# A hybrid two-layer block: split weights of the mixer and the recurrent stage kept in DRAM between the halves of the tokens

## Chip, cores and metric

The kernel runs on one core of a Trainium2 chip. The metric is the device time of one execution in microseconds (us). Engines are named PE (TensorE, with PEld for its weight loads), DVE (VectorE), ACT (ScalarE), POOL (GpSimd) and SP (SyncE, which here issues all DMAs).

## What is computed

Two layers on x of 1024 tokens by 1024 features, all in float32. Layer 0 has a mixer with two groups of heads (a gated delta rule and RWKV-7), layer 1 a gated linear recurrence; each is followed by a gated feed-forward network. Each sublayer has its norm and its AdaLN shift, scale and gate.

```python
def reference(x, c, ...):
    for layer in range(DEPTH):
        shift, scale, gate = adaln_params(c, ada_w[layer, 0], ada_b[layer, 0])
        h = rms_norm(x, norm_pre[layer, 0]) * (1.0 + scale) + shift
        if layer % 2 == 0:
            y = delta_rwkv_mixer(h, mix_w_in[j], mix_w_out[j], ...)
        else:
            y = rglru_mixer(h, lru_w_in[j], ..., lru_wa[j], ..., lru_wx[j], ..., lru_w_out[j])
        x = x + gate * rms_norm(y, norm_post[layer, 0])
        shift, scale, gate = adaln_params(c, ada_w[layer, 1], ada_b[layer, 1])
        h = rms_norm(x, norm_pre[layer, 1]) * (1.0 + scale) + shift
        y = swiglu_ffn(h, ffn_w_gate[layer], ffn_w_up[layer], ffn_w_down[layer])
        x = x + gate * rms_norm(y, norm_post[layer, 1])
    return x

def rglru_mixer(h, w_in, conv_w, conv_b, wa, ba, wx, bx, lam, w_out):
    gate_branch, xb = jnp.split(h @ w_in, 2, axis=-1)
    xb = causal_depthwise_conv(xb, conv_w) + conv_b
    r = sigmoid(einsum('btnd,nde->btne', xb, wa) + ba)
    i = sigmoid(einsum('btnd,nde->btne', xb, wx) + bx)
    ...
    return (hs * gelu(gate_branch)) @ w_out
```

## The kernel before

Every large product is done in three passes with operands split in two: a matrix w is taken as wh, its cast to the type float32r, and wl = w - wh, and the product is wh·xh + wh·xl + wl·xh, three matmuls of 128x128 by 512 columns (`gemm_steps`, or `prod` in `down`).

The weights are split in `load_w`. For each tile of 128 x 512 numbers (256 KB: four blocks of 128x128 side by side, two of 128x256, or one of 128x512) it lets SP load the raw tile into a buffer wf or wd (L135), lets ACT cast it to wh (L138), and POOL or DVE subtract to wl (L139). In the mixer POOL subtracts; in the recurrent stage DVE does it for the first tile of a product and POOL for the second; in the output products DVE does. wh and wl have three buffers each in the whole program. The raw tiles have two buffers wf in the mixer, and after `deepen` eight (two wf, six wd). A tile's buffers come free when PE has done its 12 matmuls.

The tokens go in two halves of 512, h = 0 and h = 1; each half loads and splits every weight again. The stages, in the order of time: `start` (AdaLN of the first norm), `mixer` (16 groups, a half and a head group each, of which three are at work at a time: the input products `proj` of one group, the chunk algebra of the one before, the serial chain of the one before that), the output product `mix_out` of h = 0 in the middle of the second half's groups and that of h = 1 at the end; the feed-forward stage of layer 0, both halves at once, and its product `down`; the recurrent stage `lru` with h = 0, its output through `down`, then h = 1 and its output; the feed-forward stage of layer 1. In `lru` four blocks follow one another: two input products (bank "mm"), a convolution, the two gate products with wa and wx, two products of the gate branch (bank "sb"), and the recurrence, most of it on DVE.

`proj` takes two tiles (24 matmuls), a gate product one; `down` takes one tile for each of 128 rows of the weight and each half of the columns, and `mix_out` and `lru` both use it. So the mixer has 60 input tiles and 16 output tiles in each half, and the recurrent stage 32 + 8 and 16.

Who runs what in which order on an engine is set by a scheduler that orders the recorded instructions by a model of their times; the order in the program is its starting point. Each engine, SP too, then works through its list in order: an instruction that waits holds up all behind it on that engine. Beside the weights, SP's list has loads of activations (L527), stores of results (L605), rows of AdaLN weights for the next stages (L500), and intermediate values of the feed-forward stages.

The store that the change copies exists already: the feed-forward stage puts its split product in DRAM through `gpart` (L769, L770) and loads it back with `load_g` (L804).

```python
wf = self.t(next(self.wtags), [128, step, n])[:, :m]
nc.sync.dma_start(wf, w[k0 * 128:(k0 + m) * 128, c0:c0 + n].rearrange("(k p) c -> p k c", p=128))
wh = self.t(tag or "wh", [128, step, n], F32R)[:, :m]
wl = self.t(tag or "wl", [128, step, n], F32R)[:, :m]
nc.scalar.copy(wh, wf)
(nc.gpsimd if self.pool_lo and (self.pool_lo > 1 or k0) else nc.vector).tensor_tensor(wl, wf, wh, ALU.subtract)
```

Of the kernel before, what the change touches and what calls it, by code (L numbers as in the profile page):

```python
# [10 lines left out]
F32 = mybir.dt.float32  # L11
# [4 lines left out]
ALU = mybir.AluOpType  # L16
# [4 lines left out]
KD = D // 128  # L21
# [51 lines left out]
class Block:  # L73
# [53 lines left out]
    def load_w(self, w, c0, nk=KD, n=128, tag=None):  # L127

        nc = self.nc
        step = 512 // n  # L130
        out = []
        for k0 in range(0, nk, step):
            m = min(step, nk - k0)
            wf = self.t(next(self.wtags), [128, step, n])[:, :m]
            nc.sync.dma_start(wf, w[k0 * 128:(k0 + m) * 128, c0:c0 + n].rearrange("(k p) c -> p k c", p=128))  # L135
            wh = self.t(tag or "wh", [128, step, n], F32R)[:, :m]
            wl = self.t(tag or "wl", [128, step, n], F32R)[:, :m]
            nc.scalar.copy(wh, wf)  # L138
            (nc.gpsimd if self.pool_lo and (self.pool_lo > 1 or k0) else nc.vector).tensor_tensor(wl, wf, wh, ALU.subtract)  # L139
# [40 lines left out]
    def run(self):  # L180
        nc, a = self.nc, self.a
# [12 lines left out]
        self.gd = self.dram("gd", 2 * NF * 2 * 128, 512)  # L194
        self.cd = self.dram("cd", 2 * (PRE + MID) * 128, 512)
# [380 lines left out]
    def down(self, lhs, w, h, x_in, x_out, Gb, banks, xtag="yx", tail=(None, 0), keep=False, aside=None):  # L576
# [37 lines left out]
        for half in range(2):  # L614
            ps = [self.t(banks[4 * half + t], [128, 512]) for t in range(4)]
            held = []
            for k in range(nk):
# [5 lines left out]
                wp, = self.load_w(w[k * 128:(k + 1) * 128], half * 512, 1, 512, ttag if late else None)  # L623
# [184 lines left out]
    def lru(self, h, hs):  # L808
# [16 lines left out]
        def branch(b):  # L825
            out = []
            for m in (2 * b, 2 * b + 1):
                ps = self.now(self.proj(w, 1024 + 128 * m, hs))
# [7 lines left out]
        for b in range(4):  # L836
# [5 lines left out]
            wb = [self.load_w(a[wn][0, b], 0, 2, 256) for wn in ("lru_wa", "lru_wx")]  # L842
# [8 lines left out]
            for i, m in enumerate(ms):  # L851
                z = self.t("cy", [128, 512])
                ps = self.now(self.proj(w, 128 * m, hs, "sb"))
# [24 lines left out]
    def layers(self, hs, AB, x1, x2, x3, late):  # L878
# [4 lines left out]
        for n, (l, x_in, x_out) in enumerate(subs):  # L883
# [20 lines left out]
            for h in range(2):  # L904
# [24 lines left out]
                def aside():  # L929
# [3 lines left out]
                    elif n + 1 < len(subs):  # L933
# [6 lines left out]
                               "s2" if keep else "yx", ("cy", 6) if keep else ("ht", 7) if last else (None, 0), keep, aside)  # L940
# [74 lines left out]
    def mix_out(self, h, x, x_out, mT, Gb, banks):  # L1015
# [12 lines left out]
        if h == 0:  # L1028
            self.down(lhs, self.a["mix_w_out"][0], h, x, x_out, Gb, banks)
        else:  # L1030
            return self.down(lhs, self.a["mix_w_out"][0], h, x, x_out, Gb, banks, "s2", ("cy", 6), True)
# [103 lines left out]
    def gdn_inputs(self, w, hs, i, h):  # L1135
        nc = self.nc
        out = []
        for n in range(3):
            ps = (yield from self.proj(w, 512 * n + 128 * i, hs))
# [14 lines left out]
        ps = (yield from self.proj(w, 1536 + 128 * i, hs))  # L1154
# [179 lines left out]
    def rwkv_lora(self, w, hs, h):  # L1334
        nc = self.nc
        wdad = self.shifted((yield from self.proj(w, 2056 + 1536, hs)), 24, 12, h, "st")
# [215 lines left out]
```

## Time and profile before

| | us |
|---|---|
| median of 3 runs | 2824.09 |
| lowest and highest | 2818.7, 2838.25 |
| the profiled execution | 2831.3 |
| its span in the trace | 2829.2 |

The execution's own time is 2.1 us longer than the span, which runs from the first to the last recorded instruction. All times of rows are us from the start of the span. In the profile all matmuls have line L98 or, for transposes, L101, since helpers record them; they are told apart by their tiles. A wait is named by the instruction that ended it. PEclk is the granted share of TensorE's full clock.

### The profile page before, as it was taken

Reading aid. Unit: us, or ns where it says so; the run is one execution under the profiler, and the core shown is the slowest. Engines: PE = TensorE matmul, PEld = TensorE weight load, DVE = VectorE, ACT = ScalarE, POOL = GpSimd, SP = SyncE. Lnnn points to the kernel's source line nnn. Section 1 sums busy time; section 2 is a strip of 40 time slices with the busy share of each in tenths; the row PEclk is TensorE's granted clock in tenths of the full one; section 3 lists DMA queues with packets and bytes.
Section 4 is the critical chain, followed back from the end, with each engine's and each line's share of the span. In section 5 each row is a group of like instructions: output and inputs, shape, how many; then the busy total and the mean of one; then the engine's idle time right before and its main releaser. Section 6 shows DMA issues by size and latency. Waiting matters only on the chain. (4 is left out here: it accounts for less than half of the span.)

```text
span 2829.2 us, 43760 instructions
## 1 busy us (share of the span) xinstructions
PE 2655.3 (94%) x16104; PEld 2050.8 (72%) x16104; DVE 1854.8 (66%) x3280; ACT 1258.1 (44%) x2302; POOL 662.9 (23%) x516
## 2 busy tenths in 40 slices
PE   6899999998999998899999999999998899999998
PEld 3666666666766766677888878777776688888887
DVE  5867778677677655998454463997974885544233
ACT  4555565554555535333332232664755333333222
POOL 2322221232322105232330000211215333331000
PEclk9999999999999999899999999999999999999999
DMA  7412222224511154766447874635334454448753
GB/s 236 120 44 54 61 79 61 68 56 138 159 53 53 58 186 149 223 215 209 139 145 282 291 253 126 189 116 160 112 110 150 149 195 149 142 134 287 232 187 108
DMA packets 402653, 415.75 MB, mean 147 GB/s; under 512 B 26331, under 2 KB 260606, under 8 KB 402438
## 3 DMA queue, kind: packets, MB, share of 16 engines
q1 hardware_dynamic: 402438, 412.95, 45.9%
q8 instruction: 127, 2.08, 0.3%
q14 instruction: 88, 0.72, 0.1%
HBM read 333.16 MB, written 79.69 MB: 146 GB/s over the span
## 5 line engine op out<-in xcount | busy, mean ns | idle before, releaser
L98 PE MATMUL mm<-ht,wh 128*128 128x512 f32 x1920 | 664.6, 420 | 28.6 <-ACT e L686 19.8
L98 PEld LDWEIGHTS mm<-ht,wh 128*128 128x128 f32 x1920 | 358.3, 195 | 120.1 <-ACT e L686 31.3
L98 PE MATMUL mm<-ht,wl 128*128 128x512 f32 x960 | 398.3, 416 | 13.8 <-DVE wl L139 9.0
L139 POOL TENSOR_TENSOR wl<-wf,wh 128x512 fp32r<-128x512 f32 x144 | 210.8, 1466 | 554.8 <-ACT wh L138 414.1
L138 ACT CAST wh<-wd 128x512 fp32r<-128x512 f32 x206 | 127.1, 619 | 288.7 <-PE sb L98 220.8
L138 ACT CAST wh<-wf 128x512 fp32r<-128x512 f32 x215 | 133.0, 619 | 253.5 <-PE sb L98 85.4
L660 POOL TENSOR_TENSOR wl<-wd,wh 128x512 fp32r<-128x512 f32 x99 | 131.9, 1333 | 479.3 <-ACT wh L659 447.6
L139 DVE TENSOR_TENSOR wl<-wd,wh 128x512 fp32r<-128x512 f32 x182 | 126.0, 694 | 166.5 <-ACT wh L138 164.4
L98 PEld LDWEIGHTS mm<-ht,wl 128*128 128x128 f32 x960 | 186.4, 194 | 58.9 <-DVE wl L139 10.7
L537 POOL TENSOR_TENSOR sm<-sm,dv 128x1 f32<-128x1 f32 x64 | 38.6, 612 | 504.6 <-DVE sm L535 269.1
L660 DVE TENSOR_TENSOR wl<-e,wh 128x512 fp32r<-128x512 f32 x88 | 61.6, 700 | 105.1 <-ACT wh L659 105.1
L98 PE MATMUL sa<-s,wh 128*128 128x512 f32 x392 | 122.4, 394 | 0.0
L659 ACT CAST wh<-wd 128x512 fp32r<-128x512 f32 x99 | 61.3, 621 | 130.7 <-issue 46.9
L106 ACT ACT_TABLE_LOAD x90 | 115.5, 1283 | 2.3 <-PEq L1541 0.7
L98 PEld LDWEIGHTS <-h 64*64 64x64 f16 (+1 forms) x1984 | 54.0, 107 | 81.3 <-issue 53.2
L659 ACT CAST wh<-yx 128x512 fp32r<-128x512 f32 x88 | 54.6, 621 | 127.6 <-PE sb L98 45.6
L106 ACT ACTIVATE e<-e 128x512 f32<-128x512 f32 x140 | 88.3, 631 | 49.5 <-DVE e L759 26.6
L106 ACT ACTIVATE e<-mm 128x512 f32<-128x512 f32 x120 | 71.2, 594 | 73.1 <-PE mm L98 70.2
L139 POOL TENSOR_TENSOR wl<-wd,wh 128x512 fp32r<-128x512 f32 x24 | 35.1, 1462 | 269.8 <-ACT wh L138 243.2
L139 DVE TENSOR_TENSOR wl<-wf,wh 128x512 fp32r<-128x512 f32 x71 | 48.7, 689 | 67.7 <-ACT wh L138 65.1
L98 PE MATMUL sa<-wh,p 128*128 128x512 f32 x260 | 91.5, 397 | 0.0
L98 PE MATMUL sa<-s,wl 128*128 128x512 f32 x196 | 78.4, 400 | 8.7 <-DVE wl L139 8.7
(498 smaller groups left out, 6717.9 us busy)
## 6 DMA issues: line engine op xcount, KB each, us to landing
gd<-yx SPq DMA_DIRECT2D x176, 256.0 KB
wd<-in_ffn_w_down_dram SPq DMA_DIRECT2D x132, 256.0 KB
wf<-in_mix_w_in_dram SPq DMA_DIRECT2D x120, 256.0 KB
wd<-in_ffn_w_gate_dram SPq DMA_DIRECT2D x114, 256.0 KB
wd<-in_ffn_w_up_dram SPq DMA_DIRECT2D x78, 256.0 KB
yx<-x SPq DMA_DIRECT2D x72, 256.0 KB
ad<-in_ada_w_dram SPq DMA_DIRECT2D x63, 256.0 KB
wf<-in_ffn_w_gate_dram SPq DMA_DIRECT2D x62, 256.0 KB
```

The source lines that it names most:

```text
L98: self.nc.tensor.matmul(out, lhsT=lhsT, rhs=rhs, start=start, stop=stop, skip_group_check=more)
L106: return self.nc.scalar.activation(out, in_, func, bias=bias, scale=scale)
L138: nc.scalar.copy(wh, wf)
L139: (nc.gpsimd if self.pool_lo and (self.pool_lo > 1 or k0) else nc.vector).tensor_tensor(wl, wf, wh, ALU.subtract)
L537: nc.gpsimd.tensor_tensor(r, r, self.mhalf[:, 0:1], ALU.pow)
L659: nc.scalar.copy(flat(wh), full)
L660: (eng or nc.vector).tensor_tensor(flat(wl), full, flat(wh), ALU.subtract)
```

## The change

`load_w` gets a key. On the first call with a key, column and row it splits as before, and SP stores wh and wl to a DRAM tensor pd (two rows of 128 x 512 for each tile). On a later call with the same key it allocates wh and wl alone, and SP loads them from pd: no raw tile, no cast and no subtraction. The callers in the mixer, the recurrent stage and both output products pass keys; the feed-forward weights, which are used once, have none. 132 tiles are kept.

```diff
-    def load_w(self, w, c0, nk=KD, n=128, tag=None):
+    def load_w(self, w, c0, nk=KD, n=128, tag=None, key=None):
...
-            wf = self.t(next(self.wtags), [128, step, n])[:, :m]
-            nc.sync.dma_start(wf, w[k0 * 128:(k0 + m) * 128, c0:c0 + n].rearrange("(k p) c -> p k c", p=128))
             wh = self.t(tag or "wh", [128, step, n], F32R)[:, :m]
             wl = self.t(tag or "wl", [128, step, n], F32R)[:, :m]
-            nc.scalar.copy(wh, wf)
-            (nc.gpsimd if self.pool_lo and (self.pool_lo > 1 or k0) else nc.vector).tensor_tensor(wl, wf, wh, ALU.subtract)
+            kept = self.wparts.get((key, c0, k0))
+            if kept is not None:
+                for x, r in zip((wh, wl), kept):
+                    nc.sync.dma_start(x.bitcast(F32).rearrange("p k c -> p (k c)"), r)
+            else:
+                wf = self.t(next(self.wtags), [128, step, n])[:, :m]
+                nc.sync.dma_start(wf, w[k0 * 128:(k0 + m) * 128, c0:c0 + n].rearrange("(k p) c -> p k c", p=128))
+                nc.scalar.copy(wh, wf)
+                (nc.gpsimd if self.pool_lo and (self.pool_lo > 1 or k0) else nc.vector).tensor_tensor(wl, wf, wh, ALU.subtract)
+                if key is not None:
+                    kept = []
+                    for x in (wh, wl):
+                        r = self.pd[len(self.wparts) * 256 + len(kept) * 128:][:128, :m * n]
+                        nc.sync.dma_start(r, x.bitcast(F32).rearrange("p k c -> p (k c)"))
+                        kept.append(r)
+                    self.wparts[key, c0, k0] = kept
...
+        self.pd = self.dram("pd", 132 * 256, 512)
+        self.wparts = {}
...
-                wp, = self.load_w(w[k * 128:(k + 1) * 128], half * 512, 1, 512, ttag if late else None)
+                wp, = self.load_w(w[k * 128:(k + 1) * 128], half * 512, 1, 512, ttag if late else None, key and (key, k))
...
-            wb = [self.load_w(a[wn][0, b], 0, 2, 256) for wn in ("lru_wa", "lru_wx")]
+            wb = [self.load_w(a[wn][0, b], 0, 2, 256, key=(wn, b)) for wn in ("lru_wa", "lru_wx")]
...
-    def proj(self, w, c0, hs, bank="mm"):
+    def proj(self, w, c0, hs, key, bank="mm"):
         ps = self.t(bank, [128, 512])
-        yield from self.gemm_steps(ps, self.load_w(w, c0), hs)
+        yield from self.gemm_steps(ps, self.load_w(w, c0, key=key), hs)
```

The scheduler orders all engines anew. The first place that shows it is SP's list in the first half of the recurrent stage, where the first products of the gate branch begin. Before (a name's number is the tile's; x_66 and x_69 are activations in DRAM):

```order
L135 DMA wd_18924<-in_lru_wa_dram 128x2x256
L135 DMA wd_18930<-in_lru_wx_dram 128x2x256
L527 DMA yx_18635<-x_66 128x512
L135 DMA wd_18974<-in_lru_w_in_dram 128x4x128
L527 DMA yx_18637<-x_66 128x512
L605 DMA x_69<-yx_18635 128x512
L135 DMA wd_18980<-in_lru_w_in_dram 128x4x128
L135 DMA wf_19018<-in_lru_w_in_dram 128x4x128
L605 DMA x_69<-yx_18637 128x512
```

Now, at the same place (18943 and 18951 are the parts of the first block's gate weights, 18997 those of the gate branch's first tile, 19007 the raw tile after it):

```order
L150 DMA pd<-wh_18943 128x512
L150 DMA pd<-wl_18944 128x512
L150 DMA pd<-wh_18951 128x512
L150 DMA pd<-wl_18952 128x512
L150 DMA pd<-wh_18997 128x512
L150 DMA pd<-wl_18998 128x512
L143 DMA wd_19007<-in_lru_w_in_dram 128x4x128
L143 DMA wf_19047<-in_lru_w_in_dram 128x4x128
L143 DMA wf_19055<-in_lru_w_in_dram 128x4x128
L143 DMA wd_19124<-in_lru_w_in_dram 128x4x128
L143 DMA wd_19132<-in_lru_w_in_dram 128x4x128
```

The raw tile after the gate branch's first one was loaded among activations, without a store ahead of it; now it stands behind the stores of both parts of the three tiles before it.

The second place is SP's list in the second half of the recurrent stage. Before, at its beginning, the raw tiles of ten loads in a row:

```order
L135 DMA wd_20371<-in_lru_w_in_dram 128x4x128
L135 DMA wd_20377<-in_lru_w_in_dram 128x4x128
L135 DMA wd_20422<-in_lru_w_in_dram 128x4x128
L135 DMA wd_20428<-in_lru_w_in_dram 128x4x128
L135 DMA wf_20473<-in_lru_w_in_dram 128x4x128
L135 DMA wf_20479<-in_lru_w_in_dram 128x4x128
L135 DMA wd_20524<-in_lru_w_in_dram 128x4x128
L135 DMA wd_20530<-in_lru_w_in_dram 128x4x128
L135 DMA wd_20579<-in_lru_wa_dram 128x2x256
L135 DMA wd_20585<-in_lru_wx_dram 128x2x256
```

Now, in its third block, the parts of four tiles, two DMAs for each:

```order
L140 DMA wh_21125<-pd 128x512
L140 DMA wl_21126<-pd 128x512
L140 DMA wh_21129<-pd 128x512
L140 DMA wl_21130<-pd 128x512
L140 DMA wh_21171<-pd 128x512
L140 DMA wl_21172<-pd 128x512
L140 DMA wh_21175<-pd 128x512
L140 DMA wl_21176<-pd 128x512
```

A raw load waited for one of eight raw buffers; each of these waits until PE has released one of three buffers of its kind.

## Rows read from the trace of the kernel before

**Rows 1.** The page's first part: busy us, share of the span, instructions

```profile
span 2829.2 us, 43760 instructions
...
PE 2655.3 (94%) x16104; PEld 2050.8 (72%) x16104; DVE 1854.8 (66%) x3280; ACT 1258.1 (44%) x2302; POOL 662.9 (23%) x516
```

**Rows 2.** Stretches by stage: stretch, us; busy us (instructions) by engine, clock, DMA share, GB/s

```profile
420.00:1030.00 610.00, 571.20 (x5419) 408.58 (x5417) 436.24 (x928) 315.82 (x617) 145.37 (x110) 0.97 0.30 89
...
1768.00:1895.00 127.00, 116.39 (x492) 92.72 (x491) 120.27 (x230) 89.99 (x147) 31.27 (x24) 0.97 0.50 156
1895.00:1945.00 50.00, 49.95 (x239) 40.85 (x237) 30.71 (x58) 21.97 (x42) 1.29 (x1) 1.00 0.31 96
1945.00:2085.00 140.00, 126.91 (x542) 101.80 (x541) 130.28 (x209) 88.75 (x146) 27.61 (x23) 0.96 0.45 139
...
2240.00:2310.00 70.00, 70.00 (x310) 57.97 (x309) 61.34 (x78) 24.82 (x42) 22.91 (x15) 1.00 0.60 199
```

**Rows 3.** PE's waits in the mixer, 420 to 1030 us: us, times, longest

```profile
PE sa L98 <- DVE h L1192: 7.0, 6, 1.6
...
PE mm L98 <- ACT wh L138: 1.7, 2, 0.9
...
PE sa L98 <- DVE h L1176: 1.5, 3, 0.8
```

**Rows 4.** PE's waits in the recurrent stage's second half, 1945 to 2085 us

```profile
PE sa L98 <- DVE wl L139: 6.6, 5, 3.1
PE mm L98 <- DVE wl L139: 4.7, 2, 3.9
PE mm L98 <- ACT wh L138: 1.8, 1, 1.8
```

**Rows 5.** PE's waits in the recurrent stage's first half, 1768 to 1895 us

```profile
PE mm L98 <- DVE wl L139: 4.3, 2, 3.1
PE sa L98 <- DVE wl L139: 3.3, 3, 1.4
PE sb L98 <- POOL wl L139: 1.2, 2, 0.7
PE mm L98 <- POOL wl L139: 0.9, 1, 0.9
PE mm L98 <- ACT wh L138: 0.8, 1, 0.8
```

**Rows 6.** The lines of subtraction and cast, 1945 to 2085 us: ns min/median/max

```profile
L139 DVE TENSOR_TENSOR wl<-wd,wh x21: 660/684/1780, 1947.0 to 2080.6; 128x512 fp32r<-128x512 f32 x21
L139 POOL TENSOR_TENSOR wl<-wd,wh x11: 1288/1370/1820, 1949.3 to 2067.5; 128x512 fp32r<-128x512 f32 x11
...
L138 ACT CAST wh<-wd x32: 601/612/624, 1945.2 to 2079.6; 128x512 fp32r<-128x512 f32 x32
```

**Rows 7.** Timelines of VectorE and of GpSimd near 1885 us: start, us

```profile
1885.69 0.68 DVE L860 SCALAR_TENSOR_TENSOR cy<-e,cy 128x512 f32<-128x512 f32 x1
1886.32 1.74 DVE L864 SCALAR_TENSOR_TENSOR e<-e,e 128x512 f32<-128x512 f32 x1
...
1882.86 4.65 POOL L139 TENSOR_TENSOR wl<-wf,wh 128x512 fp32r<-128x512 f32 x1 [13.56 <-ACT wh L138]
```

**Rows 8.** Timelines of SP's queue and of ScalarE near 2085 us

```profile
2084.27 0.33 SPq L135 DMA_DIRECT2D wf<-in_lru_w_out_dram  x1
...
2085.96 0.33 SPq L135 DMA_DIRECT2D wf<-in_lru_w_out_dram  x1
...
2087.18 0.62 ACT L138 CAST cy<-wf 128x512 fp32r<-128x512 f32 x1 [2.06 <-DMA wf<-in_lru_w_out_dram]
...
2089.14 0.62 ACT L138 CAST cy<-wf 128x512 fp32r<-128x512 f32 x1 [0.81 <-DMA wf<-in_lru_w_out_dram]
```

**Rows 9.** Timelines of VectorE and of PE near 1800 us

```profile
1795.22 0.68 DVE L139 TENSOR_TENSOR wl<-wd,wh 128x512 fp32r<-128x512 f32 x1
...
1801.37 0.50 PE L98 MATMUL sb<-ht,wl 128*128 128x512 f32 x1 [0.50 <-POOL wl L139]
```

More of the change, by code (lines that the diff above doesn't have):

```diff
@@ L574, in prenorm, with down @@
         return self.to_h(self.normed(x, h), A, B)
-    def down(self, lhs, w, h, x_in, x_out, Gb, banks, xtag="yx", tail=(None, 0), keep=False, aside=None):
+    def down(self, lhs, w, h, x_in, x_out, Gb, banks, xtag="yx", tail=(None, 0), keep=False, aside=None, key=None):
         nc = self.nc
@@ L827, in branch @@
             for m in (2 * b, 2 * b + 1):
-                ps = self.now(self.proj(w, 1024 + 128 * m, hs))
+                ps = self.now(self.proj(w, 1024 + 128 * m, hs, "lru"))
                 cv = self.with_tail(ps, m, h)
@@ L852, in lru @@
                 z = self.t("cy", [128, 512])
-                ps = self.now(self.proj(w, 128 * m, hs, "sb"))
+                ps = self.now(self.proj(w, 128 * m, hs, "lru", "sb"))
                 self.act(z, ps, AF.Square, scale=0.044715 ** 0.5)
@@ L939, in layers @@
                 xs = self.down(lhs, w, h, x_in, x_out, res[n]["G"], F_BANKS[4:] + F_BANKS[:4],
-                               "s2" if keep else "yx", ("cy", 6) if keep else ("ht", 7) if last else (None, 0), keep, aside)
+                               "s2" if keep else "yx", ("cy", 6) if keep else ("ht", 7) if last else (None, 0), keep, aside,
+                               "lru" if l is None else None)
                 if nxt:
@@ L1138, in gdn_inputs @@
         for n in range(3):
-            ps = (yield from self.proj(w, 512 * n + 128 * i, hs))
+            ps = (yield from self.proj(w, 512 * n + 128 * i, hs, "mix"))
             idx = 4 * n + i
@@ L1153, in gdn_inputs @@
             out.append(o)
-        ps = (yield from self.proj(w, 1536 + 128 * i, hs))
+        ps = (yield from self.proj(w, 1536 + 128 * i, hs, "mix"))
         th = self.t("e", [128, 512])
@@ L1366, in rwkv_inputs @@
         nc.vector.tensor_copy(egc, eg[:, :, 64])
-        k = self.shifted((yield from self.proj(w, 2056 + 512 + 128 * p, hs)), 12 + 4 + p, 4 + p, h, "e")
+        k = self.shifted((yield from self.proj(w, 2056 + 512 + 128 * p, hs, "mix")), 12 + 4 + p, 4 + p, h, "e")
         ss = self.head_sum(k, self.blk, cl(self.col["rwkv_k_k"]))
@@ L1381, in rwkv_inputs @@
         tt(kt, k, G, ALU.mult)
-        r = self.shifted((yield from self.proj(w, 2056 + 128 * p, hs)), 12 + p, p, h, "e")
+        r = self.shifted((yield from self.proj(w, 2056 + 128 * p, hs, "mix")), 12 + p, p, h, "e")
         tt(ar[:, :, 1, :], c8(r), eg[:, :, 1:65], ALU.mult)
@@ L1386, in rwkv_inputs @@
         self.mm(pb, self.blk, r)
-        v = self.shifted((yield from self.proj(w, 2056 + 1024 + 128 * p, hs)), 12 + 8 + p, 8 + p, h, "p")
+        v = self.shifted((yield from self.proj(w, 2056 + 1024 + 128 * p, hs, "mix")), 12 + 8 + p, 8 + p, h, "p")
         bo = self.t("p", [128, 512])
```

8 lines of the change are left out of this document (4 added, 4 removed).

## Prediction

> **What bounds the kernel now.** The page's first part says where the limit is: TensorE (PE) is busy for 2655.3 of 2829.2 us, VectorE (DVE) for 66% of the span, ScalarE (ACT) for 44%, GpSimd (POOL) for 23% [rows 1]. So 174 us of PE idle time are all that a change can win which leaves the matmuls as they are, and this one does. The second view, stretches by stage, tells which part of them lies where the change works. Its splits run in four places: the mixer's first half of the tokens (48 to 420 us), its second (420 to 1030 us, together with the first output projection), and the recurrent stage's halves, 1768 to 1895 and 1945 to 2085 us. In 420 to 1030 us PE is idle for 610 - 571.2 = 38.8 us, in 1768 to 1895 us for 10.6, in 1945 to 2085 us for 13.1 [rows 2]. The third view, PE's waits in these stretches, tells what ends them. In the mixer it is chains of VectorE (eight rows of the view, 26.0 us), and a weight part for 1.7 us only [rows 3]. In the recurrent second half it is nothing but weights: 6.6 + 4.7 + 1.8 = 13.1 us, all of its idle time [rows 4]. In the first half it is weights too, 4.3 + 3.3 + 1.2 + 0.9 + 0.8 = 10.5 us [rows 5]. There VectorE is busy for 120.3 of 127 us and in the second half for 130.3 of 140 [rows 2]: the low parts come late because they stand in VectorE's full queue.
>
> **What goes.** 132 of the weight tiles (60 and 16 of the mixer, 40 and 16 of the recurrent stage) lose their cast and subtraction in the second half. In 1945 to 2085 us the view of the two lines shows subtractions of 684 ns on VectorE, 1370 ns on GpSimd and casts of 612 ns [rows 6]. The recurrent second half alone has 24 subtractions on VectorE, 24 x 0.684 = 16.4 us out of 130.3; VectorE then has some 114 of 140 us to do and no longer holds PE up.
> Term A, PE's waits for weights in the second halves: -13.1 (recurrent) - 1.7 (mixer) = -14.8 us. Nothing of this is hidden by other work: PE is the last engine there.
> Term B, clock and pitch. The granted clock in 1945 to 2085 us is 0.96, against 1.00 in a dense stretch, where 310 matmuls take 70.00 us, 0.226 us each [rows 2]. The 542 matmuls at that pitch are 122.4 us, and PE counts 126.9 as busy: up to 4.5 us sit inside busy time. I take -3, since part of it is fill after other waits.
> The Trainium skill (Trainium Kernel Development and Optimization, section Performance Expectations) says that matmul busy time is a bad measure of the distance to the limit, because matmuls are pipelined. By that rule term B would be the whole 4.5 us and the sum 1.5 us lower; the dense row agrees that a fully busy PE here runs at its pitch.
> Term C, relief in the mixer. A subtraction on GpSimd also slows VectorE: at 1885.69 us a scalar_tensor_tensor takes 0.68 us, and the next one of the same size, begun while GpSimd's subtraction of 4.65 us runs, takes 1.74 [rows 7]. In the mixer's second half 60 such subtractions go, up to 1.06 us of VectorE time each, off chains on which PE waits 26 us. Bounds: 0, where the delays lie beside PE work, and -26; I take -4, because VectorE is busy for only 436 of 610 us there and most delays are covered.
>
> **What comes.** 264 stores of 256 KB in the first half, and 264 loads in place of 132 in the second; at 0.262 MB each that is 396 DMAs more, some 104 MB. All of it goes through SP's one queue, in order.
> Term D, second half: refill of the parts. The tiles wh and wl have three buffers each. A weight tile is 12 matmuls, 12 x 0.226 = 2.71 us, so from the moment that PE lets go of a buffer until it wants it again there are two tiles, 5.42 us. Before, a cast and a subtraction had to fit in (0.61 + 0.68 or 1.37 us); the raw weights had been fetched up to eight tiles ahead. Now two DMAs have to. From issue to use one load took 2087.18 - 2084.27 = 2.91 us and 2089.14 - 2085.96 = 3.18 us, and an issue 0.33 us [rows 8]. In 1768 to 1895 us the DMA share is 0.50 at 156 GB/s: 19.8 MB, 75.6 DMAs of 256 KB in 63.5 us of full work, 0.84 us each [rows 2]. A pair is then about 3.2 + 0.33 + 0.84 = 4.4 us: it fits with 1.0 us to spare when nothing else is queued, and each other 256 KB DMA ahead of it (activations, AdaLN weights) takes most of that. Bounds: 0, and +20 (a refill of 6.5 us makes (2.71 + 6.5) / 3 = 3.07 us a tile, 0.36 more on 56 tiles). I take +4, the clean rows being nearest. In the mixer a tile is used every 10 us (60 in 610), and the refill is covered by the other heads' matmuls.
> Term E, first half: the stores. A store of wl waits until VectorE or GpSimd has made it, and what is behind it on SP waits too: raw weight loads, activation loads for the next half, AdaLN rows. In the mixer's first half this costs little: a raw tile has two buffers, so the next load waited for the same subtraction already. In the recurrent first half it matters: before, loads ran ahead as far as eight buffers; in the new order the load of a projection's second half stands behind both stores of its first half, and other loads are two to four tiles ahead of the stores. Worked at the first such place: the low part is made at 1795.9 us, then 0.33 us for its store's issue, 3.18 from the load's issue to use, 0.61 cast and 1.37 subtraction, 1801.4 us; PE wanted it at 1800.87 [rows 6, 8, 9]: 0.5 us late with an empty queue, later with a loaded one, at each of four blocks. On top come 80 stores x 0.84 = 67 us of DMA work in 127 us, 0.53 beside the 0.50 that is there: the queues are full, and a load waits behind stores. Bounds: 0 (if DMA work slips into 1895 to 1945 us, where the share is 0.31 [rows 2]), and +67, worked out below. I take +12: four blocks x 1 to 2 us, and the 4 us by which 1.03 exceeds the stretch, with a mixer rest of 2.
>
> **Sum.** -14.8 - 3 - 4 + 4 + 12 = -5.8 us. The profiled execution took 2831.3 us, span and what lies around it: 2825.5. The median of the runs is 2824.09, 7.2 below it; so the forecast is 2818 us, -0.2%, which is no change within the about 1% that a measurement of this kernel can tell.
>
> **Rivals.**
> 1. Slower: the stores jam the recurrent first half. With eight DMAs of 256 KB in the queue (as many as there are raw buffers) a load takes 8 x 0.84 + 0.33 = 7.05 us, then cast 0.61, subtraction 1.37, two store issues 0.66: 9.7 us a step. With loads two tiles ahead that is 4.85 us a tile where it is 127 / 40 = 3.17 now, +67 us; with 2.5 ahead 3.88 us, +28. The middle, +48 for term E, gives -14.8 - 3 - 4 + 4 + 48 = +30: 2854 us. It decides from 3.62 us a tile (+18, sum zero). For it: the full DMA share and the new order of SP. Against it: PE is dense here and the three-deep ring already limits how far the parts run ahead.
> 2. Not faster at all: the ring of three cannot be refilled in time, term D at +20 eats term A: with E at +12 the sum is +10, 2834 us. For it: pairs have 1 us to spare; against it: the clean rows.
> 3. Faster: VectorE and GpSimd are what holds PE in the mixer too. C at its full -26, B at -4.5, D +2, E +3: -40, 2784 us. For it: VectorE chains end most of the mixer's waits, and the slowed row. Against it: VectorE has 174 us idle in that stretch.
> The Trainium skill (SBUF — State Buffer, section Who interferes with whom) has a rule by which rival 3 would hold: VectorE and GpSimd share a port pair, a VectorE instruction with two SBUF inputs contends with a GpSimd one that reads SBUF, and the loser blocks. The slowed instruction of rows 7 agrees; that PE waits less for it is not shown.
>
> **How the numbers follow.** Forecast 0.42, rival 1 0.22, rival 2 0.20, rival 3 0.16. Range of the forecast's own terms: 2800 to 2836. The 8-in-10 range reaches into both sides: 2788 to 2858, from just short of rival 3 to just past rival 1. Faster by over 1% (below 2796) is rival 3, its own upper tail against the forecast's lower one: 0.16. Slower by over 1% (above 2852) is most of rival 1 and the tail of rival 2: 0.22. The rest, 0.62, is within 1%.
>
> **What would show it.** Right: in the recurrent second half PE's waits for subtractions are gone, and small waits for DMAs of wh and wl stand in their place, 4 us in all; that half takes about 128 us instead of 140; the first half takes up to 12 us longer, with the cast waiting for DMAs; the mixer's second half is within 5 us. Wrong: waits for DMAs of over 15 us in either recurrent half, a mixer that moves by more than 10 us, or PE idle time in the feed-forward stages, whose work the change does not touch.

## The result, and the profile after

The changed kernel takes 2784.20 us (median of 4 runs, 2773.7 to 2791.41) against 2823.84 for the kernel before beside it: ratio 0.9852, 95% interval [0.9826, 0.9878], 1.5% faster. The forecast was 2818 us with a range from 2788 to 2858, so the gain is about 40 us where some 6 were expected. 2784 is the time of rival 3. Most of the difference lies in two terms of the forecast: the relief of the mixer (term C) and the price of the stores (term E).

The profiled execution took 2782.86 us, its span 2781.1. The page's first part, and the bytes in DRAM:

```profile
span 2781.1 us, 44135 instructions
...
PE 2639.1 (95%) x16104; PEld 2041.2 (73%) x16104; DVE 1779.6 (64%) x3224; ACT 1176.4 (42%) x2164; POOL 553.3 (20%) x440
...
HBM read 367.76 MB, written 148.90 MB: 186 GB/s over the span
```

Against [rows 1], TensorE's busy time fell by 16.2 us, so of the 48 us between the two spans some 32 were TensorE's idle time (173.9 us before, 142.0 now). VectorE does 75 us less, ScalarE 82, GpSimd 110; all that work was bought with DMA traffic.

Where the time went is read from SP's stores, which mark the same points of the work in both traces. The fifth head group of the mixer (the middle of its first half) is stored at 405.2 us before and 407.0 now; the last group at 1025.2 and 990.2. Between the two it is 620.0 us before and 583.2 now, so the mixer's second half gives 36.8 us. The first store of the recurrent first half's output comes 178.8 us after that of the feed-forward stage's second half before, 175.1 now; that of the recurrent second half another 164.7 and 154.1 us later: 3.8 and 10.6 us. From there to the first store of the last output's second half it is 692.6 and 690.0 us. The profiled execution of before took 7 us more than its median, so the spans differ by 48 us and not by 40.

The stretches by stage (columns as in [rows 2]: us; busy us of PE, PEld, DVE, ACT, POOL; clock, DMA share, GB/s). In the changed kernel the loads of parts are L140, the cast L144, the subtraction L145 and the stores L150; line numbers behind `load_w` are 15 or 16 higher.

```profile
48.00:407.00 359.00, 334.50 (x3069) 234.87 (x3068) 268.54 (x557) 202.70 (x388) 103.55 (x76) 0.97 0.48 156
420.00:995.00 575.00, 557.55 (x5394) 399.28 (x5393) 403.21 (x920) 276.69 (x548) 61.40 (x50) 0.99 0.42 139
1736.00:1860.00 124.00, 115.18 (x501) 93.00 (x499) 116.49 (x213) 81.43 (x134) 25.42 (x20) 0.99 0.86 291
1907.00:2037.00 130.00, 124.79 (x539) 101.22 (x538) 103.00 (x182) 65.13 (x104) 5.50 (x8) 0.97 0.79 259
```

In the mixer's second stretch PE is idle for 17.5 us of 575 (38.8 of 610 before, [rows 2]), and its clock is 0.99 in the place of 0.97. So of the 35 us between the two stretches 21 are idle time; the other 14 are PE's busy time (571.2 and 557.6 us), and most of these fit the clock, as 571.2 x 0.97 / 0.99 is 559.7. PE's waits there:

```profile
PE mm L98 <- POOL wl L145: 2.9, 4, 1.1
PE mm L98 <- ACT wh L144: 1.8, 2, 1.0
...
PE sb L98 <- DVE S L1522: 1.2, 2, 0.9
PE sa L98 <- DVE h L1192: 1.1, 3, 0.5
PE sb L98 <- DVE ch L1509: 1.1, 2, 0.8
PE sa L98 <- DVE h L1208: 0.9, 2, 0.7
...
PE sb L98 <- DVE s L1100: 0.9, 2, 0.4
```

The row of h L1192 of [rows 3], 7.0 us, is now h L1208 with 0.9, and the row of h L1176, 1.5 us, is h L1192 with 1.1; no row of VectorE is over 1.2. The eight rows of VectorE's chains, 26.0 us before, are where PE's idle time came back. Two of these rows end in VectorE instructions that had been slow themselves. One is the row of h L1176, now h L1192 (after the count: busy us and mean ns):

```profile
L1176 DVE TENSOR_TENSOR h<-k,s 128x512 f16<-128x512 f16 x9 | 12.8, 1423 | 0.0
L1192 DVE TENSOR_TENSOR h<-k,s 128x512 f16<-128x512 f16 x9 | 10.2, 1129 | 0.0
```

The other is that of s L1084, 3.9 us before and 0.9 now (s L1100): five tensor_tensor instructions of 128x512 with a median of 1339 ns before and 692 now. The two largest rows, h L1192 with 7.0 us and ch L1493 with 5.3, end in instructions that are as long as they were (428 and 440 ns; 220 and 224): these came late, and were not slow. Weight parts (POOL wl, ACT wh) hold PE up for 4.7 us; before it was 2.4, as a row of POOL wl with 0.7 us stood beside the 1.7 of [rows 3].

In the recurrent second half, the waits that answer to [rows 4]:

```profile
PE mm L98 <- DMA wl<-pd: 4.4, 2, 3.5
PE mm L98 <- DMA wh<-pd: 0.5, 1, 0.5
```

The 13.1 us of waits for subtractions and casts are gone, 4.9 us for the parts' loads have come. In the first half, against [rows 5]:

```profile
PE sa L98 <- DVE wl L145: 6.0, 5, 1.9
PE sb L98 <- POOL wl L145: 1.0, 1, 1.0
PE sb L98 <- ACT wh L144: 0.9, 1, 0.9
PE mm L98 <- DVE wl L145: 0.8, 1, 0.8
```

8.7 us where it was 10.5, none of them a wait for a DMA, while the DMA share rose from 0.50 to 0.86 (second view above).

### The profile page after: what moved, and what is told of

Its sections match the earlier page's. It is cut to its first block, busy times and chain, and to the rows that moved or that the text cites. A ratio compares the mean times of both kernels' runs of the same rounds, so it can differ in the third digit from the quotient of the medians.

```text
span 2781.1 us, 44135 instructions
## 1 busy us (share of the span) xinstructions
PE 2639.1 (95%) x16104; PEld 2041.2 (73%) x16104; DVE 1779.6 (64%) x3224; ACT 1176.4 (42%) x2164; POOL 553.3 (20%) x440
## 5 line engine op out<-in xcount | busy, mean ns | idle before, releaser
L98 PE MATMUL mm<-ht,wl 128*128 128x512 f32 x960 | 391.4, 409 | 9.6 <-DMA wl<-pd 4.4
L675 POOL TENSOR_TENSOR wl<-wd,wh 128x512 fp32r<-128x512 f32 x99 | 130.9, 1323 | 524.0 <-ACT wh L674 483.8
L144 ACT CAST wh<-wd 128x512 fp32r<-128x512 f32 x168 | 104.0, 620 | 263.1 <-PE sb L98 215.3
L145 DVE TENSOR_TENSOR wl<-wd,wh 128x512 fp32r<-128x512 f32 x156 | 108.1, 694 | 161.1 <-ACT wh L144 158.8
L145 POOL TENSOR_TENSOR wl<-wf,wh 128x512 fp32r<-128x512 f32 x80 | 115.6, 1453 | 290.1 <-ACT wh L144 232.0
L144 ACT CAST wh<-wf 128x512 fp32r<-128x512 f32 x133 | 82.0, 619 | 157.5 <-PE sb L98 78.4
L106 ACT ACTIVATE e<-mm 128x512 f32<-128x512 f32 x120 | 71.3, 594 | 146.0 <-PE mm L98 144.0
L674 ACT CAST wh<-wd 128x512 fp32r<-128x512 f32 x99 | 61.3, 621 | 131.0 <-PE sb L98 43.2
L1198 POOL TENSOR_TENSOR s<-s,k 128x512 f32<-128x512 f32 x16 | 24.7, 1543 | 340.0 <-DVE s L1441 163.5
L782 ACT CAST yx<-yx 128x512 fp32r<-128x512 f32 x88 | 54.6, 621 | 77.3 <-DVE yx L779 40.5
L98 PEld LDWEIGHTS sa<-s,wh 128*128 128x128 f32 x392 | 73.7, 188 | 15.5 <-issue 0.4
```

Of the source, the lines that this page charges most:

```text
L98: self.nc.tensor.matmul(out, lhsT=lhsT, rhs=rhs, start=start, stop=stop, skip_group_check=more)
L106: return self.nc.scalar.activation(out, in_, func, bias=bias, scale=scale)
L674: nc.scalar.copy(flat(wh), full)
L675: (eng or nc.vector).tensor_tensor(flat(wl), full, flat(wh), ALU.subtract)
L782: nc.scalar.copy(hi, g)
L1198: nc.gpsimd.tensor_tensor(im, first, one32, ALU.add)
```

## The experiments

Each kernel was run beside the kernel before, whose median was 2824 to 2826 us in every group. "The changed kernel" is 2784.2 us.

### Which part gave the time

Theory before the runs: the mixer's input tiles. Rivals: the recurrent stage's terms alone, or the new order of all engines.

**no_mix_in**: the mixer's input tiles get no key.

```diff
+        if key == "mix":
+            key = None
```

> The changed kernel with the mixer's 60 input tiles split in both halves again (no stores, no loads for them); output products and recurrent stage as changed. The time by stage says that the mixer's second half gave 35 us. If that is the work of the input tiles (any of the theories on it), this kernel takes 2784 + 30 to 35 = about 2816 us, and the mixer's second half is as long as before the change (about 610 us from 420 us on). If the output product's tiles or a new order of the engines gave the time, it stays at 2784 to 2795 us.

Measured 2802.94 us, ratio 0.9913 [0.9885, 0.9941]: 18.7 us given back, not 30 to 35. The part is right; its size by the stage marks was too large, since it leans on one execution of before that took 7 us more than the median. In this run's trace the mixer takes 607.1 us from the fifth group's store to the last, and PE is idle for 37.5 us of them; in the changed kernel it is 18.8 of 583.2. So the idle time differs by as much as the time of the runs.

**no_lru**: the keys of the recurrent stage are taken away instead.

```diff
+        if key is not None and key != "mix" and key[0] != "mix":
+            key = None
```

> The changed kernel with the recurrent stage (input, gate and output products) as before, so without its 56 tiles' stores and loads; the mixer as changed. By the stages of the two traces the recurrent stage gave 15 us: 2784 + 15 = 2799 us. By the forecast's terms for it (-13.1 - 3 + 4 + 10 = -2) it would be 2786 us.

Measured 2800.29 us, 0.9907 [0.9874, 0.9941]: 16.1 us given back, as by the marks (14.4), and far from the 2 of the forecast's terms.

**no_mix_out**: only the 16 output tiles of the mixer get no key.

```diff
+        if key is not None and key[0] == "mix":
+            key = None
```

> The changed kernel with the 16 tiles of the mixer's output product split in both halves again. The whole mixer's part of the gain is 2826 - 2800 = 26 us by the run without the recurrent stage's tiles, its input tiles' part 2803 - 2784 = 19; what is left for the output tiles is 7 us, where the forecast named nothing of its own for them (A had 1.7 us for the whole mixer). If they give it: 2791 us. If the 7 us are scatter of the medians: 2784 us.

Measured 2781.40 us, 0.9848 [0.9831, 0.9865]: nothing comes from them. So the mixer's input tiles gave 19 us by their own run and 26 by the run without the recurrent stage (2826 - 2800); the medians scatter by several us, and no run settles what lies between.

**stores_only**: the first halves store all parts, the second halves split as before; the forecast's term E by itself.

```diff
-            if kept is not None:
+            if False:
...
-                if key is not None:
+                if key is not None and kept is None:
```

> The kernel before with the change's stores alone: in the first halves wh and wl of all 132 tiles go to DRAM, in the second halves everything is loaded raw and split as before. This is the forecast's term E by itself. By the forecast 2824 + 12 = 2836 us (rival 1: 2872). By the trace of the changed kernel, whose recurrent first half took 4 us less than before and whose mixer's first half ended within 2 us, the stores cost nothing: 2824 within 5 us.

Measured 2827.80 us beside 2825.97, ratio 1.0003 [0.9984, 1.0023]: the stores cost nothing that can be measured, and 12 us (1.0042) lies outside. Its recurrent first half, the stretch and PE's waits:

```profile
1768.00:1895.00 127.00, 117.88 (x507) 95.43 (x507) 117.95 (x215) 82.99 (x138) 27.14 (x21) 0.97 0.85 288
```

```profile
PE sa L98 <- DVE wl L145: 6.5, 5, 2.2
PE mm L98 <- DVE wl L145: 1.4, 1, 1.4
PE sb L98 <- POOL wl L145: 1.0, 1, 1.0
PE sb L98 <- ACT wh L144: 0.3, 1, 0.3
```

The DMA share is 0.85 and the bandwidth 288 GB/s, and still the waits are like those of [rows 5] (9.2 us in all, 10.5 there), with no DMA among them.

### Which engine's work

Each of the next three puts one engine's work back into the mixer's second half.

**wl_kept**: wl from DRAM, wh by ScalarE's cast of the raw tile.

```diff
+                only = key == "mix"
                 for x, r in zip((wh, wl), kept):
-                    nc.sync.dma_start(x.bitcast(F32).rearrange("p k c -> p (k c)"), r)
+                    if only and x is wh:
+                        wf = self.t(next(self.wtags), [128, step, n])[:, :m]
+                        nc.sync.dma_start(wf, w[k0 * 128:(k0 + m) * 128, c0:c0 + n].rearrange("(k p) c -> p k c", p=128))
+                        nc.scalar.copy(wh, wf)
+                    else:
+                        nc.sync.dma_start(x.bitcast(F32).rearrange("p k c -> p (k c)"), r)
```

**wh_kept**: the mirror, wl by GpSimd's subtraction from the raw tile.

```diff
+                only = key == "mix"
+                if only:
+                    wf = self.t(next(self.wtags), [128, step, n])[:, :m]
+                    nc.sync.dma_start(wf, w[k0 * 128:(k0 + m) * 128, c0:c0 + n].rearrange("(k p) c -> p k c", p=128))
                 for x, r in zip((wh, wl), kept):
-                    nc.sync.dma_start(x.bitcast(F32).rearrange("p k c -> p (k c)"), r)
+                    if only and x is wl:
+                        nc.gpsimd.tensor_tensor(wl, wf, wh, ALU.subtract)
+                    else:
+                        nc.sync.dma_start(x.bitcast(F32).rearrange("p k c -> p (k c)"), r)
```

> The changed kernel, but for the mixer's 60 input tiles the second half loads only wl from DRAM; wh comes from the raw tile by ScalarE's cast, as before the change. GpSimd has no subtraction there, ScalarE has its 60 casts (37 us) back, DMA count is as in the changed kernel. Theory GpSimd (its subtractions slow VectorE's chains, on which TensorE waits): 2784 within 8 us, VectorE's waits small. Theory ScalarE (casts stand in its queue ahead of the chains' activations): about 2815 us. Theory of half and half: about 2800 us.

> The mirror: for the mixer's 60 input tiles the second half loads wh from DRAM and the raw tile, and GpSimd subtracts to wl; ScalarE casts nothing there. Theory GpSimd: about 2815 us, PE's waits for VectorE in the second half back at about 26 us. Theory ScalarE: 2784 within 8 us. In both the load of a second tile and the subtraction behind it may cost a few us more.

Measured 2782.34 us (0.9854 [0.9814, 0.9894]) and 2802.22 us (0.9918 [0.9891, 0.9946]). ScalarE's 60 casts cost nothing that can be measured; GpSimd's 60 subtractions alone cost all that no_mix_in gave back.

**pool_idle_sub**: the changed kernel, with subtractions that no matmul waits for.

```diff
                 for x, r in zip((wh, wl), kept):
                     nc.sync.dma_start(x.bitcast(F32).rearrange("p k c -> p (k c)"), r)
+                if key == "mix":
+                    j = self.t("wf", [128, step, n], F32R)[:, :m]
+                    nc.gpsimd.tensor_tensor(j, wh.bitcast(F32), wl, ALU.subtract)
```

> The changed kernel with 60 subtractions added on GpSimd in the mixer's second half, one behind each pair of loaded parts, of the same size and types as the removed ones, into a buffer that nobody reads. No matmul waits for them. Theory that GpSimd's reads and writes of SBUF slow VectorE, or that they hold up GpSimd's own chain steps: 2784 + 20 to 30 = about 2810 us, VectorE's busy time in that stretch up by 20 us or more. Theory that the weights' own path (load, cast, subtraction) made TensorE late: 2784 within 8 us.

Measured 2800.77 us, 0.9914 [0.9883, 0.9945]: 16.6 us for work whose result nobody reads. No matmul waits for that work, so the path of the weights is not the reason. The same 570 us of the mixer and VectorE's costliest group in them, first of the changed kernel:

```profile
420.00:990.00 570.00, 552.55 (x5372) 395.14 (x5371) 402.44 (x919) 276.69 (x548) 61.40 (x50) 0.99 0.42 138
```

```profile
L1092 DVE SCALAR_TENSOR_TENSOR e<-e,cols,e 128x512 f32<-128x512 f32 x36 | 26.9, 748 | 4.9 <-ACT e L106 4.6
```

and of pool_idle_sub (the group is the same line of the code, three lines further down):

```profile
420.00:990.00 570.00, 539.88 (x5263) 384.83 (x5262) 420.26 (x884) 272.12 (x538) 144.72 (x110) 0.98 0.39 129
```

```profile
L143 POOL TENSOR_TENSOR wf<-wh,wl 128x512 fp32r<-128x512 f32 x60 | 84.2, 1404 | 219.2 <-DMA wl<-pd 205.8 <-DMA x<-yx 13.2
```

```profile
L1095 DVE SCALAR_TENSOR_TENSOR e<-e,cols,e 128x512 f32<-128x512 f32 x36 | 32.7, 908 | 4.0 <-ACT e L106 3.7
```

With 35 fewer instructions VectorE is busy for 420.3 us in the place of 402.4, and 36 equal instructions take 908 ns each in the place of 748. PE's waits for VectorE are back with it, where no such row of the changed kernel is over 1.2 us (h L1211 is h L1208 there, ch L1512 is ch L1509):

```profile
PE sa L98 <- DVE ar L1402: 5.1, 1, 5.1
PE sb L98 <- DVE ch L1512: 4.4, 5, 2.2
PE sa L98 <- DVE h L1211: 2.7, 4, 1.5
```

One place where VectorE is slowed, GpSimd's timeline and then VectorE's:

```profile
423.00 1.58 POOL L143 TENSOR_TENSOR wf<-wh,wl 128x512 fp32r<-128x512 f32 x1 [0.22 <-DMA wl<-pd]
```

```profile
422.79 0.68 DVE L1398 TENSOR_TENSOR p<-e,e 128x512 f32<-128x512 f32 x1
423.39 1.75 DVE L1400 TENSOR_TENSOR p<-e,e 128x512 f32<-128x512 f32 x1
```

Two instructions of one form and size, 0.68 us and, begun under GpSimd's subtraction, 1.75: the picture of [rows 7], now made at will. (In [rows 7] the first of the two VectorE instructions began under GpSimd's too and was not slowed, while GpSimd's took 4.65 us, where 1.37 is the median in [rows 6]: there GpSimd's instruction was long as well.)

### What of GpSimd's work: what it reads, or its queue

**pool_memset**: the unread subtraction of pool_idle_sub becomes a memset, which reads nothing.

```diff
-                    j = self.t("wf", [128, step, n], F32R)[:, :m]
-                    nc.gpsimd.tensor_tensor(j, wh.bitcast(F32), wl, ALU.subtract)
+                    j = self.t("wf", [128, step, n])[:, :m]
+                    nc.gpsimd.memset(j, 0.0)
```

> The changed kernel with 60 memsets of 128x512 on GpSimd in the mixer's second half in the place of the unread subtractions of the run before. A memset reads nothing from SBUF. Theory port (VectorE is slowed by GpSimd's reads beside its own): 2784 within 6 us, VectorE's instructions as short as in the changed kernel. Theory queue (any work on GpSimd makes its own chain steps late): about 2800 us if a memset takes 1.4 us, in proportion less if it is shorter. Theory of any access: also about 2800 us, with VectorE slowed.

Measured 2789.50 us, 0.9858 [0.9819, 0.9898], between the two. GpSimd's memsets and VectorE's group as above:

```profile
L143 POOL MEMSET wf<- 128x512 f32 x43 | 20.4, 524 | 0.1
```

```profile
L1095 DVE SCALAR_TENSOR_TENSOR e<-e,cols,e 128x512 f32<-128x512 f32 x36 | 27.0, 749 | 4.9 <-ACT e L106 4.7
```

A memset takes 0.52 us, and 17 of the 60 ran before this stretch, so GpSimd was not occupied as long as by subtractions: a queue theory would give 60 x 0.524 / 84.2 x 16.6 = 6 us, and 5 were seen. VectorE was not slowed (749 ns). Inconclusive on the time.

**pool_small**: two subtractions of 128x1 behind each pair, in the place of the full one of pool_idle_sub.

```diff
-                    j = self.t("wf", [128, step, n], F32R)[:, :m]
-                    nc.gpsimd.tensor_tensor(j, wh.bitcast(F32), wl, ALU.subtract)
+                    j = self.t("wf", [128, step, n])[:, :m]
+                    for i in range(2):
+                        nc.gpsimd.tensor_tensor(j[:, i, 0:1], wh[:, i, 0:1].bitcast(F32), wl[:, i, 0:1].bitcast(F32), ALU.subtract)
```

> The changed kernel with two subtractions of 128x1 on GpSimd behind each of the 60 pairs of loaded parts in the mixer's second half, into a buffer that nobody reads. A subtraction of 128x1 takes 0.6 us in the trace, so GpSimd is occupied for about 60 x 1.2 = 72 us at the same times as by the unread full-size subtractions (84 us), but reads next to nothing. The memsets (31 us in all, some of them early) could not tell the two apart. Theory port: 2784 within 6 us, VectorE not slowed. Theory queue: the 16.6 us of the unread subtractions in proportion, 72 / 84 x 16.6 = +14: 2798 us.

Measured 2783.97 us, 0.9841 [0.9800, 0.9883]. But two such subtractions took 0.26 us each here, not 0.6: 28.6 us in all, too little to decide.

**pool_small5**: the same with five (`range(5)`, five neighbouring columns).

> As the run with two small subtractions, but five of 128x1 behind each pair: two took 0.26 us each, 28.6 us in all and not the 72 expected, so that run did not occupy GpSimd enough to tell port from queue. Five are 60 x 5 x 0.26 = 79 us, as much as the unread full-size subtractions (84 us). Theory port: 2784 within 6 us and VectorE's busy time near 400 us in 420 to 990 us. Theory queue: +16 us, 2800 us, as with the full-size ones.

Measured 2778.23 us, 0.9845 [0.9819, 0.9872].

```profile
420.00:990.00 570.00, 550.56 (x5399) 391.59 (x5399) 397.58 (x919) 278.14 (x551) 132.07 (x351) 0.99 0.42 137
```

```profile
L144 POOL TENSOR_TENSOR wf<-wh,wl 128x1 f32<-128x1 f32 x300 | 70.5, 273 | 224.8 <-DMA wl<-pd 224.3 <-POOL h L1200 0.3 <-POOL wf L144 0.2
```

```profile
L1096 DVE SCALAR_TENSOR_TENSOR e<-e,cols,e 128x512 f32<-128x512 f32 x36 | 26.9, 748 | 4.1 <-ACT e L106 3.8
```

GpSimd is busy for 132 us, nearly as long as in pool_idle_sub (145), again behind each pair of loads, and nothing is lost: VectorE stands at 397.6 us and 748 ns. The queue theory falls. What costs is the reading of a full tile beside VectorE. By the Trainium skill (SBUF — State Buffer, section Who interferes with whom) a VectorE instruction with two SBUF inputs contends with a GpSimd instruction that reads SBUF and not with one that only writes it, and whoever comes second blocks. The subtractions and the memsets agree: VectorE's group takes 908 ns beside the one and 749 beside the other. Beside the small subtractions, which read too but last 0.27 us each, it takes 748 ns; how long one of these holds VectorE up no run shows.

### GpSimd's subtractions elsewhere

If the subtraction on GpSimd is the harm, the first half and the kernel before can be rid of it without DRAM.

**mix_half**: in the mixer, VectorE takes the first tile of each product.

```diff
-                (nc.gpsimd if self.pool_lo and (self.pool_lo > 1 or k0) else nc.vector).tensor_tensor(wl, wf, wh, ALU.subtract)
+                (nc.gpsimd if self.pool_lo and k0 else nc.vector).tensor_tensor(wl, wf, wh, ALU.subtract)
```

> The changed kernel, but in the mixer (its first half and the output product of h = 0) half of the subtractions go from GpSimd to VectorE: each product's first tile, as in the recurrent stage. 30 subtractions of 1.45 us leave GpSimd, 30 of 0.69 us come to VectorE in 372 us of which it is busy for 280. Theory port with the gain of the second half (19 us for 60 subtractions, 0.3 us each): the first half gets 30 x 0.3 = 9 us shorter at most, less what 21 us more on VectorE's chains cost: 2775 to 2784 us. Theory that VectorE's own work is the limit there: 2790 to 2800 us.

Measured 2765.01 us, 0.9779 [0.9740, 0.9817]: 19 us better than the changed kernel, twice the 9 us that were expected at most.

**before_half**: the same line, put into the kernel before.

> The kernel before, nothing in DRAM, with one line changed: in the mixer the first tile of each product is subtracted on VectorE, the second on GpSimd, in both halves. If GpSimd's subtractions are what made the mixer slow: the first half gains what it gained in the changed kernel (19 us) and the second about half of the 19 us that its 60 input tiles cost, less VectorE's 21 us of new work: 2825 - 19 - 5 = about 2800 us. If the gain of the change needs the second split gone, or VectorE is the limit: 2820 us or more.

Measured 2794.01 us, 0.9878 [0.9837, 0.9920]: one line, without any DRAM copy, gives 32 of the change's 40 us.

**mix_dve**: no subtraction of the mixer on GpSimd (there `pool_lo` is 2, in the recurrent stage True).

```diff
+                (nc.gpsimd if self.pool_lo is True and k0 else nc.vector).tensor_tensor(wl, wf, wh, ALU.subtract)
```

> The changed kernel with all of the mixer's remaining subtractions (60 of the first half, 16 of its output product) on VectorE, none on GpSimd. If GpSimd's reads are all that counts, the next half gives what the first gave, 19 us: 2746 us. If VectorE's own work takes over as the limit (60 x 0.69 = 41 us on 280 of 372 us busy): 2765 to 2790 us. I expect the second, 2765 to 2775.

Measured 2756.84 us, 0.9744 [0.9695, 0.9792]: 8 us less than mix_half, with overlapping intervals, and faster than the 2765 to 2775 that were expected. To the store of the fifth group, which comes at 384.2 us, in the place of 407.0:

```profile
48.00:384.00 336.00, 325.60 (x3062) 230.14 (x3063) 263.43 (x611) 202.38 (x386) 21.85 (x18) 0.99 0.52 166
```

Beside the first row of the second view above (359 us to the same point): VectorE has 54 instructions more, about 54 x 0.69 = 37 us of subtractions, and is busy for 263.4 us in the place of 268.5. What it gained by being left alone is more than what it took over.

**dve_no_mix**: as mix_dve, but the mixer's weights not in DRAM at all.

```diff
+        if key is not None and (key == "mix" or key[0] == "mix"):
+            key = None
```

> No part of the mixer's weights in DRAM (recurrent stage as changed), and all of the mixer's subtractions on VectorE in both halves, none on GpSimd. It tells whether the mixer's gain needs the DRAM copies at all. If GpSimd's subtractions beside VectorE were the whole of it: within 5 us of the kernel that has the copies and VectorE's subtractions (2757 us). If the second split itself costs (60 x 0.69 = 41 us of VectorE, 60 x 0.62 = 37 us of ScalarE): 2765 to 2775 us.

Measured 2765.04 us, 0.9787 [0.9764, 0.9810]: once GpSimd is out, the mixer's copies in DRAM are worth 8 us by the medians (the intervals overlap), not 19 to 26.

### The ring of three

In the changed kernel, SP's queue around PE's longest wait for a part (start, us), and PE's row:

```profile
1925.75 1.64 SPq L620 DMA_DIRECT2D x<-yx  x2
1927.44 0.42 SPq L542 DMA_DIRECT2D yx<-x  x1
1928.40 0.32 SPq L620 DMA_DIRECT2D x<-yx  x1
1928.77 0.96 SPq L542 DMA_DIRECT2D yx<-x  x2
1929.84 0.40 SPq L140 DMA_DIRECT2D wl<-pd  x1
```

```profile
1934.98 0.80 PE L98 MATMUL mm<-ht,wl 128*128 128x512 f32 x1 [3.50 <-DMA wl<-pd]
```

The load of wl is issued at 1929.84 us behind activations, and the matmul that waits for it starts 5.1 us later. And PE's clock in five stretches around the wait:

```profile
1925.00:1930.00 5.00, 4.13 (x22) 3.22 (x20) 4.93 (x8) 1.14 (x2) 0.00 (x0) 1.00 0.86 320
1930.00:1934.50 4.50, 1.19 (x3) 0.30 (x2) 3.24 (x8) 0.13 (x1) 0.00 (x0) 0.96 0.84 269
1934.90:1938.00 3.10, 3.02 (x7) 2.45 (x8) 2.51 (x5) 0.00 (x0) 0.00 (x0) 0.50 0.83 274
1938.00:1942.00 4.00, 4.00 (x13) 2.98 (x13) 0.00 (x0) 0.00 (x0) 0.00 (x0) 0.63 0.75 256
1942.00:1946.00 4.00, 4.00 (x19) 3.33 (x18) 1.61 (x3) 2.15 (x4) 0.00 (x0) 1.00 0.75 243
```

After 3.50 us of idle time the granted clock falls from full to half (2.4 to 1.2 GHz) and stays there to about 1941 us: 7 + 13 matmuls take 7.1 us, which at [rows 2]'s 0.226 us each would be 4.5. The wait costs 3.5 + 2.6 = 6.1 us.

**combo**: mix_half, and in the recurrent second half every second tile's parts go to the raw buffers wd, which are idle there: six pairs in turn. **dve_ring**: mix_dve with the same. **ring_more**: the changed kernel with that alone.

```diff
-            wh = self.t(tag or "wh", [128, step, n], F32R)[:, :m]
-            wl = self.t(tag or "wl", [128, step, n], F32R)[:, :m]
             kept = self.wparts.get((key, c0, k0))
+            more = None
+            if kept is not None and key != "mix" and key[0] != "mix":
+                self.turn = 1 - self.turn
+                more = "wd" if self.turn else None
+            wh = self.t(tag or more or "wh", [128, step, n], F32R)[:, :m]
+            wl = self.t(tag or more or "wl", [128, step, n], F32R)[:, :m]
...
+        self.turn = 0
```

> The kernel with half of the mixer's subtractions on VectorE (2765 us), and in the recurrent second half every second tile's parts in the raw buffers that are idle there, so that six pairs of buffers are in turn in the place of three. The forecast's term D (the ring of three is refilled late) measured 4.9 us of PE's waits for parts in the changed kernel: if the ring is the cause, 2760 us, and the waits are gone; if the loads are late for SP's order or for the DMA load, 2765.

> All of the mixer's subtractions on VectorE (2757 us) together with the six pairs of buffers in the recurrent second half (12 us in the run before, 2765 to 2753, where 5 were expected from TensorE's waits). If the two add up: 2745 us. If the buffers' 12 us were in part scatter: 2752 us.

> The changed kernel with nothing but the six pairs of buffers in the recurrent second half. The two runs that had them beside another edit gave 12 and 8 us. Forecast by the waits for parts (4.9 us) and by the matmuls at half the clock behind the longest of them (13 at 0.43 in the place of 0.23 us, 2.6 us): 2784 - 7.5 = 2776.5 us.

Measured 2753.09 us (0.9733 [0.9690, 0.9776]), 2748.48 (0.9738 [0.9715, 0.9760]) and 2775.46 (0.9826 [0.9797, 0.9855]): 12, 8 and 9 us less than without the deeper ring, in each pair with overlapping intervals. The traces agree better: from the first output store of the recurrent first half to that of the second it takes 155.0 us in mix_half and 146.0 in combo, 154.2 in mix_dve and 146.2 in dve_ring, 154.1 in the changed kernel and 145.9 in ring_more. The recurrent second half of ring_more:

```profile
1907.00:2030.00 123.00, 122.98 (x548) 101.06 (x547) 102.96 (x182) 64.77 (x104) 5.40 (x8) 1.00 0.83 280
```

No idle time is left and the clock is 1.00, so the ring was what made the parts late. dve_ring, which beats both kernels, is 2.6% faster than the kernel before; it and combo are equal within their intervals.

## Why the prediction was wrong

**Where PE waits (right).** The reading of [rows 3 to 5] holds: PE waited for VectorE's chains in the mixer and for weight parts in the recurrent halves. The waits in the mixer and in the recurrent second half went; those of its first half, which still splits, stayed (8.7 us). What the forecast had as a sign of being wrong came true: the mixer moved by more than 10 us. What it had as a sign of being right came true as well: the recurrent second half is 10.6 us shorter, where its terms A, B and D make -12.1 there.

**Term A, -14.8 (right in the recurrent half).** Its 13.1 us are gone, and no other subtraction is late there. The mixer's 1.7 us did not go: waits for weight parts there are 4.7 us now, 2.4 before.

**Term B, -3 (right in kind).** PE's busy time there fell by 2.1 us (126.9 to 124.8, or 0.234 to 0.232 us a matmul), and by 3.9 (0.224 us a matmul) when ring_more took the last waits: the 4.5 us of the bound were nearly all there to be had, but only with no wait left. What the forecast left out is the mixer, where the clock rose from 0.97 to 0.99; how much of that belongs to the one execution of before no run tells.

**Term C, -4 (the step that failed).** It was mis-sized: the mechanism of [rows 7] was right, and it measured -19 us (no_mix_in; -17 and -18 by pool_idle_sub and wh_kept). That is some 15 of the 34 us by which the sum was off. The forecast took -4 "because VectorE is busy for only 436 of 610 us there and most delays are covered". The share of an engine says nothing of delays on a chain: PE's idle time lay behind VectorE's chains, on which some instructions were slowed and others came late, and the rows of PE's waits had put 26 us there. That each of the late ones stood behind a slowed one is argued; what is shown is that they are late with GpSimd's full subtractions and in time without them (pool_idle_sub and the changed kernel). Rival 3 read it that way. Its -26 is the upper end, and what the kernel gave by pool_idle_sub and no_mix_in is two thirds of it. So it is partly luck that the sum of rival 3 meets the measured time: its A, B and C promise more than came, its E (+3) and the 3.8 us of the recurrent first half, for which it has no term, made up for it.

**Term D, +4 (half right).** The waits are 4.9 us, the longest at a load that is late behind activations, as the forecast had it. But a wait was priced at its own length; the deeper ring takes away 8 to 9 us, and behind the wait of 3.5 us the clock falls. So the term should have been twice as large.

**Term E, +12 (the other step that failed).** It measured 1.8 us with an interval on both sides of zero (stores_only): another 10 of the 34 us. The mechanism exists (in the changed kernel's first half ScalarE's cast once waited 3.1 us for a raw load, and PE 0.9 us for the cast), but in sum PE's waits did not grow: it waits for weights for 9.2 us in stores_only and 8.7 in the changed kernel, 10.5 before. The DMA work was mis-sized too: 80 stores were to come on top of the 0.50 at 0.84 us each, 67 us. The share rose from 0.50 of 127 us to 0.86 of 124, from 63.5 to 106.6 us, so by 43 us. SP issues 75 DMAs in that stretch before and 140 now: 79 stores came and 14 loads went elsewhere. That is 65 DMAs more and about 0.66 us each. Rival 1 (48 us) falls with it. The 3.8 us by which this half got shorter no term explains. With the stores alone (stores_only) it is 177.2 us, 1.7 shorter in one execution; the rest no run took apart.

**Sum.** With what was measured, -13.1 + 4.9 - 2.1 for the recurrent second half, -3.8 for the first and -19 to -26 for the mixer make -33 to -40; the medians say -40. What is open is the recurrent first half and whether the mixer's part is nearer to 19 or to 26.

## What to carry to other kernels

An engine that is idle a quarter of the time can still set the end: add up the waits that the bound engine spends on its chains, and ask what makes these instructions long (equal instructions with two durations), before any busy share. Look then for the cheapest way to remove the cause: here VectorE took over all of the mixer's subtractions (dve_no_mix, 2765 us), and that gave more than to spare GpSimd those of the second half through DRAM (the changed kernel, 2784), though VectorE was the fuller engine. Price a wait of the bound engine with the matmuls at half clock behind it, and a DMA with a share measured under load.

## What was not expected of the hardware

GpSimd's subtraction of a full tile slows VectorE so much that VectorE, with 37 us of subtractions more, was busy for 5 us less once GpSimd had none. GpSimd occupied for 70 us by 300 small subtractions cost nothing. A wait of 3.50 us was followed by some 6 us at half clock. And the DMA engines moved 288 to 291 GB/s at shares of 0.85 and 0.86 in the recurrent first half, where 21 MB of some 36 are stores of weight parts, and no matmul waited for a DMA there.
